# First feed-forward product of a hybrid attention block as a 2x2 block product with seven block multiplications

## The chip, the cores and the metric

The kernel runs on one NeuronCore of a Trainium2 chip (trn2). The metric is the device time of one execution in microseconds (us). Engines are named as in the profile: PE is the matrix engine (PEld its weight load), DVE the vector engine, ACT the scalar engine, POOL the GpSimd engine, SP the engine that only issues DMAs. All matmul operands are float32 or float32r (a float32 rounded to what PE multiplies in one pass).

## The reference, cut to what matters

One step of a block over 640 tokens (128 context tokens and 512 latent tokens) of width 1024: a mixer with two groups of heads, then a feed-forward part with a squared ReLU, then a final norm. Conditioning vectors give a shift, a scale and a gate per condition (context tokens have one, latent tokens the other).

```
h = rmsnorm(x, norm1_w) * (1 + sc1) + sh1
y, new_states = mixer(h, ...)                  # ends in a product with w_out
x = x + g1 * y
h = rmsnorm(x, norm2_w) * (1 + sc2) + sh2
x = x + g2 * (jnp.square(jax.nn.relu(h @ w_ff1)) @ w_ff2)   # w_ff1 1024x4096, w_ff2 4096x1024
out = rmsnorm(x, final_norm_w)
```

## The kernel before, in words

**Precision.** Each float32 matrix is held as a high part (rounded to float32r) and a low part (the rest). A product is three matmuls, high by high, high by low and low by high (`three`, lines 147 to 150). ACT makes the high part by a copy, DVE the low part by a subtraction (`split_l`, line 104). For weights this is done in `fetch` (121 to 139): an SP load of 512 KB into a staging tile `st` (two buffers), ACT writes `wh`, DVE writes `wl`. `weights` (141 to 145) runs that three tiles ahead of use, at high priority, over the list `todo` (109 to 118).

**Stages.** Until about 375 us the mixer; its last part is the product with w_out in four blocks of 256 output rows (loop at line 1011): each block's sums are added to the residual `xr` (1017), squared into `sq2` (1022) and scaled into `hH` and `hL` (1025, 1026), the high and low parts of the feed-forward input, 8 tiles k of 128 features by 640 tokens, plus two columns that hold the shift sh2 of the two conditions. The dots that give sh2 and later g2 are done by DVE (`ada_dot`, 961 to 969) on rows that POOL's queue loads.

**Feed-forward.** `ff1(f)` (1045 to 1065) makes tile f of 32 of the hidden layer: two PSUM banks, of 384 and of 258 columns, each with 8 k by 3 matmuls; DVE multiplies by the row norm `r2` (1057), ACT does ReLU with the shift as bias, the square and the high part, DVE the low part (1064). `ff2` (1098 to 1107) takes four hidden tiles at a time: for 5 token tiles by 2 halves one bank of 512 columns with 4 by 3 matmuls; `acc_y` (1109) adds each bank into `y` by DVE, 80 banks in all. At group 6 the sum is multiplied by g2 and added to the residual in token layout, `xt` (1116, 1117); group 7 goes through `last` (1120 to 1135), which also does the final norm and the stores. `to_tokens` (1074) turns the residual by PE transposes after tile 3.

**Order of the work.** The order on each engine comes from the framework's planner, which simulates the program and takes what is ready by priority; work marked high priority goes first. Each engine then runs its list strictly in order. Banks come from two pools, `bank` (3) and `xbank` (5 in this part). Weight tiles: 3 buffers each for high and low in `whp`, `wlp`, and 2 more of each in `whp2`, `wlp2` for the feed-forward part.

Of the kernel before, what the change touches and what calls it, by code (L numbers as in the profile page):

```python
# [19 lines left out]
P = 128  # L20
D = 1024
# [4 lines left out]
SPANS = ((0, 384), (384, 640))  # L26
CONDS = ((0, 0, P), (1, P, T))
# [23 lines left out]
def hybrid_step(ctx: ExitStack, tc: tile.TileContext, I, O):  # L51
# [909 lines left out]
    def ada_dot(g, ft, after=None):  # L961
        st = stp.tile([P, 1024], F32, tag="sta", name="stg")
        nc.gpsimd.dma_start(out=st, in_=I["adag"][0 if g == SH2 else 1, ft])
        for n in range(2):
            a = AB[:, g, ft, n:n + 1]
            i = stt(out=cr[:, 2, :], in0=st, scalar=1.0, in1=cr[:, n, :], op0=ALU.mult, op1=ALU.mult, accum_out=a)  # L966
            if after is not None:
                behind(i.ins, after)
            tt(out=a, in0=a, in1=cb[:, CB_BA + 8 * g + ft:CB_BA + 8 * g + ft + 1], op=ALU.add)
# [26 lines left out]
    sq2 = ffp.tile([P, T], F32, name="sq2")  # L996
# [8 lines left out]

    for k in range(KT):
        ada_dot(SH2, k)
        dve.tensor_copy(hH[:, k, T:T + 2], AB[:, SH2, k, :])
        split_l(hL[:, k, T:T + 2], AB[:, SH2, k, :], hH[:, k, T:T + 2])

    for b in range(4):
# [8 lines left out]
        for f in range(2):  # L1020
            k = 2 * b + f
            square_add(sq2, xr[:, k, :], k, 0, T)
            for c, p0, p1 in CONDS:
                a2 = AB[:, SC2, k, c:c + 1]
                act(hH[:, k, p0:p1], xr[:, k, p0:p1], AF.Copy, scale=a2)
                stt(out=hL[:, k, p0:p1], in0=xr[:, k, p0:p1], scalar=a2, in1=hH[:, k, p0:p1].bitcast(F32),
                    op0=ALU.mult, op1=ALU.subtract)
    r2 = ffp.tile([P, T], F32, name="r2")
    v2 = ffp.tile([P, T], F32, name="v2")
    for lo, hi in SPANS:  # L1030
        ps = xbank("ssq")
        sum_mm(ps, (sq2,), lo, hi)
        rstd_all(ps, r2, v2, sq2, lo, hi)
# [11 lines left out]
    def ff1(f):
        gh = ff.tile([P, T], F32R, tag="gh", bufs=6, name="gh")
        gl = ff.tile([P, T], F32R, tag="gl", bufs=6, name="gl")
        wh, wl = weights()
        u = ffp.tile([P, T], F32, tag="u", bufs=2, name="u")
        ub = sm.tile([P, 2], F32, tag="ub", name="ub")  # L1050
        for hf, (lo, hi) in enumerate(FSP):
            ps = (xbank if f < 4 and f % 2 else bank)("ff1")
            for k in range(KT):
                three(ps[:, 0:hi - lo], wh[:, k * P:(k + 1) * P], wl[:, k * P:(k + 1) * P],
                      hH[:, k, lo:hi], hL[:, k, lo:hi], k == 0, k == KT - 1)
            h_ = min(hi, T)
# [189 lines left out]
```

## Time and profile before

| | us |
|---|---|
| median of 3 runs | 839.74 |
| lowest and highest run | 837.88, 840.19 |
| the profiled execution, its own time | 838.31 |
| its span, first to last instruction | 836.5 |
| granted clock of PE, mean over the span | 0.991 of full speed |

The span is 1.81 us shorter than the time of the same execution; the rest lies before the first and after the last instruction. Busy times count an engine as busy while at least one of its instructions is in flight; matmuls overlap one another, so the mean duration of one matmul is longer than the distance between two.

### The profile page before, as it was taken

Reading aid. Unit: us, or ns where it says so; the run is one execution under the profiler, and the core shown is the slowest. Engines: PE = TensorE matmul, PEld = TensorE weight load, DVE = VectorE, ACT = ScalarE, POOL = GpSimd, SP = SyncE. Lnnn points to the kernel's source line nnn. Section 1 sums busy time; section 2 is a strip of 40 time slices with the busy share of each in tenths; the row PEclk is TensorE's granted clock in tenths of the full one; section 3 lists DMA queues with packets and bytes.
Section 4 is the critical chain, followed back from the end, with each engine's and each line's share of the span. In section 5 each row is a group of like instructions: output and inputs, shape, how many; then the busy total and the mean of one; then the engine's idle time right before and its main releaser. Section 6 shows DMA issues by size and latency. Waiting matters only on the chain.

```text
span 836.5 us, 14721 instructions
## 1 busy us (share of the span) xinstructions
PE 811.4 (97%) x6022; PEld 727.3 (87%) x6022; DVE 517.3 (62%) x1008; ACT 375.4 (45%) x734; POOL 62.4 (7%) x88
## 2 busy tenths in 40 slices
PE   6999999999999999999999999999999999999995
PEld 2787688999987899999989989899899898998984
DVE  4668897868565569997305837644254343447747
ACT  5456458466454576446624405226054052250432
POOL 1121000030253003000000000000000000000000
PEclk9899999999999999999999999999999999999998
DMA  9925424141252073564103415223042041230303
GB/s 347 356 78 189 166 79 152 52 127 53 64 139 64 2 252 102 166 197 142 52 25 126 153 48 158 96 76 101 26 127 76 8 144 50 76 102 26 101 1 126
DMA packets 28436, 92.50 MB, mean 111 GB/s; under 512 B 3649, under 2 KB 4561, under 8 KB 28113
## 3 DMA queue, kind: packets, MB, share of 16 engines
q1 hardware_dynamic: 21024, 71.61, 25.6%
q0 software_dynamic: 3936, 12.15, 5.3%
q10 hardware_dynamic: 3408, 7.80, 2.7%
q8 instruction: 47, 0.77, 0.4%
q14 instruction: 21, 0.16, 0.1%
HBM read 88.31 MB, written 3.20 MB: 109 GB/s over the span
## 4 chain that ended last, share of the span: by engine, by line
PE 87%; DVE 7%; ACT 2%; DMA 2%; issue 1%; SPq 0%; DVEq 0%; ACTq 0%
PE ff L150 18%; PE ff L148 18%; PE ff L149 18%; PE ada L233 2%; PE pt L150 2%; PE pt L149 2%; PE pt L148 2%; PE pn L894 2%; PE pn L899 1%; PE ob L150 1%; PE ob L149 1%; PE ob L148 1%; PE vb L150 1%; PE vb L148 1%; PE vb L149 1%
## 5 line engine op out<-in xcount | busy, mean ns | idle before, releaser
L83 ACT ACTIVATE wh<-st 128x1024 fp32r<-128x1024 f32 (+1 forms) x90 | 92.2, 1037 | 253.3 <-PE ff L150 134.5
L148 PE MATMUL ff<-hH,wh 128*128 128x258 f32 (+1 forms) x512 | 159.1, 311 | 0.0
L150 PE MATMUL ff<-hH,wl 128*128 128x258 f32 (+1 forms) x512 | 158.9, 311 | 0.0
L149 PE MATMUL ff<-hL,wh 128*128 128x258 f32 (+1 forms) x512 | 158.8, 310 | 0.0
L105 DVE TENSOR_TENSOR wl<-st,wh 128x1024 fp32r<-128x1024 f32 x86 | 105.7, 1232 | 80.7 <-ACT wh L83 80.2
L149 PE MATMUL ff<-wl,gh 128*128 128x512 f32 x320 | 124.6, 390 | 0.0
L148 PE MATMUL ff<-wh,gh 128*128 128x512 f32 x320 | 124.5, 389 | 0.0
L150 PE MATMUL ff<-wh,gl 128*128 128x512 f32 x320 | 124.3, 389 | 0.0
L149 PEld LDWEIGHTS ff<-hL,wh 128*128 128x128 f32 x512 | 96.6, 189 | 0.3
L148 PEld LDWEIGHTS ff<-hH,wh 128*128 128x128 f32 x512 | 96.3, 188 | 0.3
L150 PEld LDWEIGHTS ff<-hH,wl 128*128 128x128 f32 x512 | 96.5, 189 | 0.0
L1114 DVE TENSOR_TENSOR y<-ff,y 128x512 f32<-128x512 f32 x60 | 41.4, 691 | 78.2 <-PE ff L150 78.2
L150 PEld LDWEIGHTS ff<-wh,gl 128*128 128x128 f32 x320 | 60.1, 188 | 12.6
L148 PEld LDWEIGHTS ff<-wh,gh 128*128 128x128 f32 x320 | 60.1, 188 | 12.3
L149 PEld LDWEIGHTS ff<-wl,gh 128*128 128x128 f32 x320 | 60.1, 188 | 12.2
L1057 DVE TENSOR_TENSOR u<-ff,r 128x384 f32<-128x384 f32 x64 | 31.2, 488 | 48.4 <-PE ff L150 48.4
L149 PE MATMUL pt<-wl,hH 128*128 128x256 f32 x160 | 46.0, 288 | 0.2 <-DVE wl L105 0.2
L150 PE MATMUL pt<-wh,hL 128*128 128x256 f32 x160 | 45.6, 286 | 0.0
L148 PE MATMUL pt<-wh,hH 128*128 128x256 f32 x160 | 45.4, 286 | 0.0
L83 ACT ACTIVATE u<-u,ub 128x128 f32<-128x128 f32 x64 | 32.3, 552 | 19.9 <-DVE ub L1059 19.7
L105 DVE TENSOR_TENSOR gl<-u,gh 128x640 fp32r<-128x640 f32 x32 | 26.3, 823 | 22.9 <-ACT gh L83 22.8
L966 DVE SCALAR_TENSOR_TENSOR cr<-stg,cr 128x1024 f32<-128x1024 f32 x32 | 38.9, 1216 | 0.0
(361 smaller groups left out, 1613.3 us busy)
## 6 DMA issues: line engine op xcount, KB each, us to landing
st<-in_wff_dram SPq DMA_DIRECT2D x64, 512.0 KB, 3.5
sta<-in_ada_dram SPq DMA_DIRECT2D x32, 512.0 KB, 6.6
st<-in_win_dram SPq DMA_DIRECT2D x18, 512.0 KB, 3.7
stg<-in_adag_dram POOLq DMA_DIRECT2D x16, 512.0 KB, 3.8
st<-in_wout_dram SPq DMA_DIRECT2D x8, 512.0 KB, 3.6
xT<-in_xT_dram SPq DMA_DIRECT2D x8, 320.0 KB, 6.4
sb<-gdr POOLq DMA_DIRECT2D x20, 128.0 KB, 3.4
xr<-in_xT_dram ACTq DMA_DIRECT2D x8, 320.0 KB, 5.1
```

The costliest lines, as they stand in the source:

```text
L83: ins = nc.scalar.activation(out, in_, func, **kw)
L105: return (eng or dve).tensor_tensor(out=dst, in0=src, in1=hi.bitcast(F32), op=ALU.subtract)
L148: mm(out, lhsT=ah, rhs=bh, start=start, stop=False)
L149: mm(out, lhsT=ah, rhs=bl, start=False, stop=False)
L150: mm(out, lhsT=al, rhs=bh, start=False, stop=stop)
L233: mm(pa[32 * i:32 * i + 32, 0:n], lhsT=sc[:, 4 * rnd + i, :], rhs=sts[i // m][:, n * (i % m):n * (i % m) + n], start=(rnd == 0), stop=(rnd ...
L894: mm(o[h2], lhsT=sbs[z][:, (2 * h2 + p) * P:(2 * h2 + p + 1) * P], rhs=vb[:, c, 2 * p + h2, :], start=True, stop=(c == 0))
L899: mm(o[h2], lhsT=qw[r, z, p, (c - 1) * P:c * P], rhs=C[j][r, 2 * z + p, :], start=False, stop=True)
L966: i = stt(out=cr[:, 2, :], in0=st, scalar=1.0, in1=cr[:, n, :], op0=ALU.mult, op1=ALU.mult, accum_out=a)
L1057: tt(out=u[:, lo:h_], in0=ps[:, 0:h_ - lo], in1=r2[:, lo:h_], op=ALU.mult)
L1114: tt(out=y[:, c, s], in0=ps, in1=y[:, c, s], op=ALU.add)
```

## The change

The 1024x4096 matrix w_ff1 is cut in two along the input features and in two along the output features, and the input in two along the features and in two along the tokens (320 each, the upper half with the two shift columns). Hidden tiles p and p+16 form a pair. Instead of eight block products there are seven, with sums and differences of blocks as operands (Winograd's form of Strassen's scheme). `prod` is one of them: 4 k by 3 matmuls of 320 or 322 columns.

- **Input side.** The scaled input is first written as float32 (`hf`), then split; four combinations T1 to T4 are made by DVE differences over 4 tiles of 322 columns, each with a high part by ACT and a low part by DVE. T1 is made after the second block of the product with w_out, the others after the last.
- **Weight side, per pair.** `sums_of` loads both tiles and makes by DVE four sums of 512 columns; `unit` splits five of them (S1, S2, S3, A22, S4), each into a buffer of its own of which there is one. The two direct blocks A11 and A12 come by `direct`: a DMA from POOL that writes the rounded tile, an ACT copy with factor -1, and a second DMA that adds the loaded tile to it. For pair 0 they are made by ACT and DVE as before.
- **Products.** Three banks a, b, c per pair. Between products DVE (and once ACT) reads a bank whose sum then goes on growing: m2 after the first product into b, m3 after the second, and m3 again from c.
- **Second product.** `ff2` runs per pair, so a bank takes 2 by 3 matmuls instead of 4 by 3, and 160 banks are added into `y` instead of 80. Its weights are made by `second` from the same staging tiles and the same three weight buffers; `whp2` and `wlp2` are gone.
- **Start.** The first two products of pairs 0, 1 and 2 (`head`, and A12 by B21) come ahead of the norm's sum and of `to_tokens`.
- **Residual.** `to_tokens` stores to DRAM; after group 14 a POOL DMA adds it into `y`. `last` runs on `y`.
- **Small.** `ada_dot` writes its products as bfloat16 to a scratch tile in the feed-forward part, and the bias is added once per vector (`ada_bias`) instead of 16 times.

```
-    for f in range(32):
-        todo.append((I["wff1"][f], None))
-        if f % 4 == 0 and f > 0:
-            todo += [(I["wff2"][f - 4 + i], None) for i in range(4)]
-    todo += [(I["wff2"][28 + i], None) for i in range(4)]
...
+    def sums_of(p, out):
+        s1 = stp.tile([P, 1024], F32, tag="st", name="s1")
+        load(s1, I["wff1"][p])
+        s2 = stp.tile([P, 1024], F32, tag="st", name="s2")
+        load(s2, I["wff1"][p + 16])
...
+        s3 = stp.tile([P, 1024], F32, tag="sta", name="s3")[:, 0:512]
+        tt(out=s3, in0=s1[:, a], in1=s2[:, a], op=ALU.subtract)
+        tt(out=s2[:, a], in0=s2[:, a], in1=s2[:, b], op=ALU.add)
+        tt(out=s1[:, a], in0=s2[:, a], in1=s1[:, a], op=ALU.subtract)
+        tt(out=s1[:, b], in0=s1[:, b], in1=s1[:, a], op=ALU.subtract)
+        return [("S1", s2[:, a]), ("S2", s1[:, a]), ("S3", s3)], (s2[:, b], s1[:, b])
...
+    def unit(pool, name, src):
+        h = pool.tile([P, 512], F32R, tag=name + "h", name=name + "h")
+        l = pool.tile([P, 512], F32R, tag=name + "l", name=name + "l")
+        act(h, src, AF.Copy)
+        split_l(l, src, h)
+        return h, l
...
+    def direct(p):
+        with tc.high_priority():
+            wh = whp.tile([P, 1024], F32R, tag="wh", name="wh")
+            wl = wlp.tile([P, 1024], F32R, tag="wl", name="wl")
+            in_order(nc.gpsimd.dma_start(out=wh, in_=I["wff1"][p]))
+            act(wl, wh.bitcast(F32), AF.Copy, scale=-1.0)
+            in_order(nc.gpsimd.dma_start(out=wl, in_=I["wff1"][p], accum_op=ALU.add))
...
+    def prod(ps, A, B, start):
+        n = B[0].shape[2]
+        for k in range(4):
+            s = slice(k * P, (k + 1) * P)
+            three(ps[:, 0:n], A[0][:, s], A[1][:, s], B[0][:, k, :], B[1][:, k, :], start and k == 0, k == 3, skip=True)
...
+    def head(p, w):
+        a = xbank("pa") if p < 3 else bank("pa")
+        u = us[p % 3]
+        prod(a, w["A11"], B11, True)
+        act(u[:, LO], a[:, LO], AF.Copy)
+        return a, u
...
+    def ff1(p, w, early=None):
+        a, u = early or head(p, w)
...
+        first = [(b, "S2", T2), (c, "S1", T1)]
+        for ps, s, t_ in (first[::-1] if p == 0 else first):
+            prod(ps, w[s], t_, True)
+        tt(out=m2, in0=b[:, 0:HE], in1=u, op=ALU.add)
+        prod(b, w["S3"], T3, False)
+        tt(out=m3, in0=b[:, 0:HE], in1=u, op=ALU.add)
+        tt(out=m3, in0=c[:, 0:HE], in1=m3, op=ALU.add)
+        if not early:
+            prod(a, w["A12"], B21, False)
+            tt(out=z0[:, LO], in0=a[:, LO], in1=r2[:, LO], op=ALU.mult)
+        prod(c, w["S4"], B22, False)
+        tt(out=m2, in0=c[:, 0:HE], in1=m2, op=ALU.add)
+        tt(out=z0[:, HALF:T], in0=m2[:, LO], in1=r2[:, HALF:T], op=ALU.mult)
+        g0 = finish(z0, p, p, m2)
+        prod(b, w["A22"], T4, False)
+        tt(out=z1[:, HALF:T], in0=m3[:, LO], in1=r2[:, HALF:T], op=ALU.mult)
+        tt(out=z1[:, LO], in0=b[:, LO], in1=u[:, LO], op=ALU.add)
+        tt(out=z1[:, LO], in0=z1[:, LO], in1=r2[:, LO], op=ALU.mult)
+        g1 = finish(z1, p, p + 16, m3)
...
+    for p in range(3):
+        w = direct(p) if p else w0
+        a, u = head(p, w)
+        prod(a, w["A12"], B21, False)
+        heads[p] = (a, u)
...
+    for p in range(1, 17):
+        if p < 16:
+            w1 = {}
+            last_unit(w1, combined(p, w1))
+            if p >= 3:
+                w1.update(direct(p))
+            g[p] = ff1(p, w1, heads.get(p))
...
+        w2 = second(p - 1)
+        ff2(p - 1, g.pop(p - 1), w2, acc_y(p - 1) if p < 16 else last)
```

## Rows read from the trace of the kernel before

**Rows 1.** The page's head and part 1: busy us, share of the span, instructions.

```profile
span 836.5 us, 14721 instructions
PE 811.4 (97%) x6022; PEld 727.3 (87%) x6022; DVE 517.3 (62%) x1008; ACT 375.4 (45%) x734; POOL 62.4 (7%) x88
```

**Rows 2.** Busy time by stretch: us, busy (instructions) per engine, clock, DMA share, GB/s.

```profile
340.00:374.70 34.70, 34.70 (x241) 34.70 (x240) 33.32 (x85) 14.42 (x28) 3.17 (x6) 1.00 0.58 180
374.70:420.00 45.30, 45.30 (x306) 44.06 (x305) 25.23 (x46) 29.77 (x47) 0.00 (x0) 1.00 0.32 101
...
500.00:600.00 100.00, 100.00 (x575) 92.24 (x574) 52.80 (x91) 33.92 (x46) 1.06 (x2) 1.00 0.32 100
```

**Rows 3.** The page's chain that ended last, by line.

```profile
PE ff L150 18%; PE ff L148 18%; PE ff L149 18%; PE ada L233 2%; PE pt L150 2%; PE pt L149 2%; PE pt L148 2%; PE pn L894 2%; PE pn L899 1%; PE ob L150 1%; PE ob L149 1%; PE ob L148 1%; PE vb L150 1%; PE vb L148 1%; PE vb L149 1%
```

**Rows 4.** PE's timeline: start us, duration us; start of the feed-forward, and at 471.

```profile
374.69 0.33 PE L148 MATMUL ff<-hH,wh 128*128 128x384 f32 x1
...
377.85 0.28 PE L148 MATMUL ff<-hH,wh 128*128 128x258 f32 x1
...
379.89 0.29 PE L150 MATMUL ff<-hH,wl 128*128 128x258 f32 x1
...
471.23 0.40 PE L148 MATMUL ff<-wh,gh 128*128 128x512 f32 x1
...
475.80 0.39 PE L150 MATMUL ff<-wh,gl 128*128 128x512 f32 x1
```

**Rows 5.** DVE's groups, 374 to 836 us: count, busy us, mean ns, idle before.

```profile
L105 DVE TENSOR_TENSOR wl<-st,wh 128x1024 fp32r<-128x1024 f32 x62 | 75.6, 1223 | 62.0 <-ACT wh L83 61.7
L1114 DVE TENSOR_TENSOR y<-ff,y 128x512 f32<-128x512 f32 x60 | 41.4, 691 | 78.2 <-PE ff L150 78.2
L105 DVE TENSOR_TENSOR gl<-u,gh 128x640 fp32r<-128x640 f32 x32 | 26.3, 823 | 22.9 <-ACT gh L83 22.8
L966 DVE SCALAR_TENSOR_TENSOR cr<-stg,cr 128x1024 f32<-128x1024 f32 x16 | 19.5, 1218 | 0.0
L1057 DVE TENSOR_TENSOR u<-ff,r 128x384 f32<-128x384 f32 x32 | 17.8, 555 | 18.3 <-PE ff L150 18.3
L1057 DVE TENSOR_TENSOR u<-ff,r 128x256 f32<-128x256 f32 x32 | 13.5, 421 | 30.2 <-PE ff L150 30.2
```

**Rows 6.** DVE's timeline, 775 to 780 us: a bank read behind a weight split.

```profile
775.74 0.69 DVE L1114 TENSOR_TENSOR y<-ff,y 128x512 f32<-128x512 f32 x1 [0.58 <-PE ff L150]
...
777.80 1.22 DVE L105 TENSOR_TENSOR wl<-st,wh 128x1024 fp32r<-128x1024 f32 x1
778.94 0.68 DVE L1114 TENSOR_TENSOR y<-ff,y 128x512 f32<-128x512 f32 x1
779.54 1.22 DVE L105 TENSOR_TENSOR wl<-st,wh 128x1024 fp32r<-128x1024 f32 x1
```

**Rows 7.** The page's DMA issues: count, KB each, median us to landing.

```profile
sta<-in_ada_dram SPq DMA_DIRECT2D x32, 512.0 KB, 6.6
...
stg<-in_adag_dram POOLq DMA_DIRECT2D x16, 512.0 KB, 3.8
```

**Rows 8.** ACT's and DVE's timelines at the hand-over from w_out to the feed-forward.

```profile
369.84 1.06 ACT L83 ACTIVATE wh<-st 128x1024 fp32r<-128x1024 f32 x1 [2.12 <-PE woc L149]
...
377.36 0.71 ACT L83 ACTIVATE hH<-xr,AB 128x512 fp32r<-128x512 f32 x1
...
378.46 0.74 DVE L1026 SCALAR_TENSOR_TENSOR hL<-xr,AB,hH 128x512 fp32r<-128x512 f32 x1
```

**Rows 9.** Busy time by stretch at the end; columns as in rows 2.

```profile
799.60:808.60 9.00, 9.00 (x41) 7.44 (x41) 1.32 (x3) 2.50 (x4) 0.00 (x0) 1.00 0.01 2
808.60:826.95 18.35, 18.34 (x81) 14.84 (x80) 16.69 (x41) 7.40 (x26) 0.00 (x0) 1.00 0.23 86
826.95:836.50 9.55, 0.00 (x0) 0.00 (x0) 5.30 (x14) 1.21 (x5) 0.00 (x0) 0.71 0.29 110
```

**Rows 10.** DVE's timeline: the last instruction of the kernel on it.

```profile
831.77 1.42 DVE L1134 SCALAR_TENSOR_TENSOR xt<-xt,r_r,g2r 128x512 f32<-128x512 f32 x2
```

More of the change, by code (lines that the diff above doesn't have):

```diff
@@ L959, in silu_rows, with ada_dot @@
         return cr
-    def ada_dot(g, ft, after=None):
+    def ada_dot(g, ft, cr, junk, after=None):
         st = stp.tile([P, 1024], F32, tag="sta", name="stg")
@@ L1022, in hybrid_step @@
             square_add(sq2, xr[:, k, :], k, 0, T)
+            hk = hf[k // 4][:, k % 4, :]
             for c, p0, p1 in CONDS:
[L1024 to L1027, printed above, removed]
-    r2 = ffp.tile([P, T], F32, name="r2")
[L1029 to L1033, printed above, removed]
@@ L1034, in hybrid_step @@
-    opst.close()
+                act(hk[:, p0:p1], xr[:, k, p0:p1], AF.Copy, scale=AB[:, SC2, k, c:c + 1])
+            n = HALF if k < 4 else T
+            act(hH[:, k, 0:n], hk[:, 0:n], AF.Copy)
+            split_l(hL[:, k, 0:n], hk[:, 0:n], hH[:, k, 0:n])
+        if b == 1:
+            t1 = first_difference()
+        if b == 3:
+            with tc.high_priority():
+                w0 = {}
+                first = sums_of(0, w0)
+    r2 = ffp.tile([P, T], F32, name="r2")
+    v2 = ffp.tile([P, T + 4], F32, name="v2")
@@ new lines, in combined, with last_unit @@
+    def combined(p, out):
+        with tc.high_priority():
+            order_, rest = sums_of(p, out)
+            for name, src in order_:
+                out[name] = unit(sp, name, src)
+        return rest
+    def last_unit(out, src):
+        with tc.high_priority():
+            out["A22"] = unit(ff, "A22", src[0])
+            out["S4"] = unit(ff, "S4", src[1])
+    with tc.high_priority():
+        for name, src in first[0]:
+            w0[name] = unit(sp, name, src)
+    s4 = first[1]
@@ L1041, in hybrid_step @@
-    FSP = ((0, 384), (384, T + 2))
-    splits = []
[L1045 to L1056, printed above, removed]
-            tt(out=u[:, lo:h_], in0=ps[:, 0:h_ - lo], in1=r2[:, lo:h_], op=ALU.mult)
-            if hf == 1:
-                dve.tensor_copy(ub, ps[:, T - lo:T + 2 - lo])
-        for c, p0, p1 in CONDS:
-            act(u[:, p0:p1], u[:, p0:p1], AF.Relu, bias=ub[:, c:c + 1])
-        act(u, u, AF.Square)
-        act(gh, u, AF.Copy)
-        splits.append(split_l(gl, u, gh).ins)
-        return gh, gl
@@ L1067, in hybrid_step, with in_order @@
-    cr = ff.tile([P, 3, 1024], F32, tag="rows", name="cr")
-    nc.scalar.dma_start(out=cr[:, 0:2, :], in_=crd.unsqueeze(0).to_broadcast([P, 2, D]))
-    xt = ff.tile([P, NT, D], F32, name="xt")
-    def wide(name):
-        return ff.tile([P, 512], F32, tag="wide", bufs=2, name=name)
+    assert not todo and not ready
+    issued = []
+    def in_order(ins):
+        if issued:
+            behind(ins.ins, issued[-1])
+        issued.append(ins.ins)
+    def direct(p):
+        with tc.high_priority():
+            wh = whp.tile([P, 1024], F32R, tag="wh", name="wh")
+            wl = wlp.tile([P, 1024], F32R, tag="wl", name="wl")
+            in_order(nc.gpsimd.dma_start(out=wh, in_=I["wff1"][p]))
+            act(wl, wh.bitcast(F32), AF.Copy, scale=-1.0)
+            in_order(nc.gpsimd.dma_start(out=wl, in_=I["wff1"][p], accum_op=ALU.add))
+        w = [(wh[:, 512 * i:512 * i + 512], wl[:, 512 * i:512 * i + 512]) for i in range(2)]
+        return {"A11": w[0], "A12": w[1]}
@@ new lines, in second @@
+    def second(p):
+        out = []
+        with tc.high_priority():
+            for f in (p, p + 16):
+                st = stp.tile([P, 1024], F32, tag="st", name="st2")
+                load(st, I["wff2"][f])
+                wh = whp.tile([P, 1024], F32R, tag="wh", name="wh")
+                wl = wlp.tile([P, 1024], F32R, tag="wl", name="wl")
+                act(wh, st, AF.Copy)
+                split_l(wl, st, wh)
+                out.append((wh, wl))
+        return out
+    def prod(ps, A, B, start):
[3 more added lines that the diff above has]
+            three(ps[:, 0:n], A[0][:, s], A[1][:, s], B[0][:, k, :], B[1][:, k, :], start and k == 0, k == 3, skip=True)
@@ L1096, in cond, with ff2 @@
         return 0 if c == 0 else 1
-    def ff2(g, gs, evac):
-        w = [weights() for i in range(4)]
+    def ff2(g, gs, w, evac):
         for c in range(NT):
```

153 lines of the change are left out of this document (111 added, 42 removed).

## Prediction

> **What bounds the kernel now.** I start with the page's busy line: PE is busy 97% of the span, DVE 62%, ACT 45% [rows 1]. A share over the whole span says nothing of one stage, so the busy times by stretch come next: from 374.7 to 420 us PE is busy for all 45.3 us, and from 500 to 600 us for all 100, at full clock, with DVE at 53% [rows 2]. In the w_out stage before it DVE is nearly full as well (33.3 of 34.7 us) and PE still never stops [rows 2]. The chain that ended last is PE's feed-forward matmuls for 54% of the span [rows 3]. So from 374.7 us to the end of the matmuls at about 826.95 the time is the number of matmuls times the distance between two of them, and that distance must be read from starts, not durations. On PE's timeline 18 matmuls of 384 columns lie between 374.69 and 377.85, so 0.1756 us each; 17 of 258 columns between 377.85 and 379.89, 0.120 us each; 20 of 512 columns between 471.23 and 475.80, 0.2285 us each [rows 4]. Check: 32 tiles x 24 x (0.1756 + 0.120) = 227.0 us and 960 x 0.2285 = 219.4 us make 446.4 of the 452.3 us; the norm's sums and the transposes fill the remaining 5.9. There is no idle time to win, only work to remove, and each matmul removed is worth its full distance as long as PE stays fed.
>
> **The removed matmuls.** The first product had 32 x 2 x 24 = 1536 matmuls; it gets 16 pairs x 7 x 12 = 1344, of 320 or 322 columns. No row has that width. Between the rows of 258 and 384 columns, 320 gives 0.120 + 62/126 x 0.0556 = 0.1474 us and 322 gives 0.1482; with three products of the one and four of the other the mean is 0.148 [rows 4]. So 1344 x 0.148 = 198.9 us against 227.0: **28.1 us less**. The bounds are the two rows themselves at equal cost per column (0.457 and 0.465 ns): 197.1 to 200.6, a saving of 26.4 to 29.9. The second product keeps 960 matmuls of 512 columns, and the transposes stay.
>
> The Trainium skill (TensorE: Matmul & The Clock Gate, "Back-to-back issue gap") gives N/2.4 + 2.5 ns between matmuls, 216 ns for 512 columns where the rows show 228; as an estimate by that page the saving would be 26.1 us and the sum 2 us higher. The row decides, since it holds what these float32r streams really do.
>
> **DVE in the steady part.** What the removed matmuls cost is on DVE. The mean of a 1024-column split is 1.223 us, of a 512-column read of a bank 0.691 [rows 5]. Back to back they take about 0.08 us less: a split started at 777.80 and the next operation, a read, at 778.94, so 1.14, and the one after it at 779.54, so 0.60 [rows 6]. Per pair: four sums and five splits of 512 columns, 9 x 0.60 = 5.4; two splits of w_ff2 tiles, 2.3; nine reads and products of 320 columns at about 0.40 (between 0.421 and 0.555 less 0.08), 3.6; two splits of 640 columns at 0.74, 1.5; ten banks added to y, 6.0, twice as many as before per hidden tile. That is 18.8 us, and 21.2 in the eight pairs with an `ada_dot` (2 x 1.22) [rows 5, 6]. PE needs 84 x 0.148 + 60 x 0.2285 = 26.1 us per pair. DVE goes from 53% to 72 to 81%: not the bound by throughput. ACT's splits, reads and ReLUs per pair cost less than DVE's and nobody reads a bank through ACT but for u, with three products between; I cost them at nothing; if ACT fell behind, the weights would be late next.
>
> **The new waits on DVE.** Before, PE never needed DVE except to free one of eight banks. Now S3 by T3 may start only when DVE has read b for m2, and S4 by B22 only when DVE has made both steps of m3. One product of 12 matmuls, 1.78 us, lies in between each time. m2 needs 0.4 to 0.5 plus whatever DVE is in the middle of: a read that PE had ready at 775.74 + 12 x 0.2285 = 778.48 started at 778.94, behind a split [rows 6]. With one such split ahead (up to 1.22) m2 ends at 1.7, just covered; m3 needs about 0.9, so 2.1 in that case, 0.3 late. Behind a waiting matmul stands all of PE. If there is never a split ahead the wait is 0, if two long operations stand ahead of each read it is about 1 for m2 and 1.4 for m3. The planner puts weight splits first, but they are few (a 1.14 us split twice in 26 us), so I take 0.2 us a pair, **3 us**, with bounds 0 and 16 (1 us a pair) in the range.
>
> **Weight buffers.** The steady loop has one buffer per combined block and three weight tiles. A direct block's tile is free after A12 by B21 of the pair before; then come two products (3.6 us) and a second product (13.7), 17.3 us in all, for POOL's DMA, ACT's copy of 1.06 and the adding DMA. No row shows a DMA that rounds or adds. The nearest is POOL's plain load of the same 512 KB, 3.8 us; the longest 512 KB row is 6.6, from the crowded start [rows 7]. The copy's 1.06 is a row as well [rows 8]. Two at 3.8 with the copy make 8.7, two at 6.6 make 14.3: hidden at both ends. The staging tiles go round within about 16 of the 26.1 us by the same prices. Free at both ends, then, with 3 us in reserve at the worse.
>
> **The start.** Before, the feed-forward began 0.1 us after the last w_out matmul on features that were ready, and the last input split ended at 379.2 [rows 8]; tiles 0 to 4 could all run ahead. Now pair 0 has 12 matmuls on ready features and 6 more on tiles 4 and 5 (2.7 us); transposes and S1 by T1 can fill, if the planner places them there. An extra ACT copy of 0.7 stands in the chain to the last split, so B21 is whole at about 380. Pair 1's weight tile comes free in the middle of the last w_out block (ACT's next use of one waited for that until 369.84 [rows 8]), so it is ready at about 379; pair 2's at the end of the block, 374.7 + 8.7 + 1 for the issues = 384.4, or 390 at the slow price. PE's work up to the first product on T2 is 72 + 12 matmuls and the 5.9 us of the balance above, 18.3 us, so until 393; DVE's (the old work left after 374.9, three differences and three splits of 1288 columns at 1.43, sums and splits, 8 operations of the norm) comes to some 22 us, ending at 397, of which the first parts are the urgent ones. Pairs 0 to 2 also lack A12 by B21 as a cover: two reads of about 0.9 us for m3 each, and 0.5 for m2 in pair 0, are exposed, 3.2 us. If second products or transposes fill all of this the cost is 0; if pair 2 and T2 come late as well, 9. I take 3.2 + 1.8 = **5 us**.
>
> **The tail.** The last second product had 120 matmuls, and DVE's work on its banks (scaling, adding, the norm) fitted beside them: from the first finished bank at 808.6 DVE was busy 16.69 + 5.30 = 22.0 us, ending at 833.19 [rows 9, 10]. Now the last product has 60 matmuls, 13.7 us, and the same 22.0 us on DVE. With its start as zero, the first bank ends at 1.4 (banks one after the other) or 4.1 (the first halves of five banks taken first, since the second weight tile is free only as the product before ends); then 22.0, then about 0.9 idle in the last norm and 3.3 from the last DVE operation to the end of the span. The end comes at 27.6 to 30.3, that is 13.9 to 16.6 after the last matmul, against 9.55 now: 4.4 to 7.1 us, I take **5.5**.
>
> **The sum.** 838.31 - 28.1 + 3 + 5 + 5.5 = 823.7 for the profiled execution. The median is 1.4 higher, so **825** for the runs. A measurement of this kernel can tell about 0.3%, 2.5 us, from no change.
>
> **The rivals.**
> - *All but the tail is hidden.* The planner has fillers for every gap, since it already mixes tiles when k 6 and 7 are late. 838.31 - 28.1 + 4.4 = 814.6, 816 on the median's scale; 812 at the upper saving of 29.9. For it: PE's unbroken 45.3 us at the old start [rows 2]. Chance 0.22.
> - *The start and the first pairs cost 9 us and the steady waits 7.* 838.31 - 28.1 + 9 + 7 + 5.5 = 831.7, or 833. The steady loop fills only after the first two pairs, each load waiting for the buffer before. Chance 0.13.
> - *DVE is late in every pair, and the kernel is slower.* The place is m2 and m3: each read behind a run of weight sums or splits (high priority, four sums in a row are 2.4 us). With 1.8 us a pair, 29 us, the time is 838.31 - 28.1 + 29 + 10.5 = 849.7, or 851. It decides from (28.1 - 10.5)/16 = 1.1 us a pair on. For it: the 0.46 us by which a read came late at half the load [rows 6]. Against: 5 us of DVE in each 26 are free. The Trainium skill (PSUM — Partial Sum Buffer, "Engine vs sequencer instructions") calls VectorE's queue strict FIFO; the trace agrees, as no read overtakes a split there. Chance 0.15, of which 0.05 end within 2.5 us of no change.
> - *The adding DMA is slow.* At 10 us each, the chain of a direct block is 21 + 1 for issues, 4.8 us beyond its 17.3, in 13 pairs: 62 us, 888. No row speaks for it. Chance 0.05.
>
> **How the numbers follow.** The forecast keeps 0.45, with its own range 819 to 831. Faster: 0.22 + 0.13 + 0.45 = 0.80; same 0.05; slower 0.15. The range starts at 813, near the lower end of the first rival, and ends at 843, where the bounds of the start (9), the steady waits (16) and the tail (7.1) meet: 838.31 - 28.1 + 32.1 + 1.4 = 843.7.
>
> **What would show it.** The chain should still be PE, with 1344 matmuls of 320 and 322 columns 0.148 us apart. PE's idle time before S3 and S4 products, put down to m2 and m3, should total some 3 us from pair 3 on and 3 in the first pairs. DVE should be at 72 to 81% of a stretch in the middle, and the span should end 14 to 17 us after the last matmul. PE idle on `wl` of a direct block would prove the buffers' sum wrong; over 1.1 us idle a pair on m2 or m3 would prove the forecast wrong altogether; a distance well above 0.148 would take the saving itself.

## The result, and the profile after

The changed kernel takes **843.98 us** (median of 5 runs, 843.51 to 844.67) against 839.74 for the kernel before beside it: ratio 1.0055, 95% interval 1.004 to 1.007. It is slower by 4 us where I forecast 15 us faster, and it lies 1 us above the range of 813 to 843. The profiled execution has a span of 842.4 us and took 844.21.

The page's head, part 1 and the chain by line, beside [rows 1, 3]:

```profile
span 842.4 us, 14750 instructions
...
PE 798.6 (95%) x5830; PEld 704.8 (84%) x5830; DVE 641.9 (76%) x1200; ACT 416.3 (49%) x827; POOL 88.3 (10%) x123
...
PE ff L145 9%; PE ff L146 8%; PE ff L147 8%; PE pb L145 3%; PE pb L147 3%; PE pb L146 3%; PE pc L145 2%; PE pc L146 2%; PE pa L147 2%; PE pc L147 2%; PE pa L145 2%; PE pa L146 2%; PE pt L146 2%; PE pt L147 2%; PE pt L145 2%
```

The matmuls went (6022 to 5830 is exactly the 192), PE was 13 us less busy, and the span still grew. So PE no longer worked all the time. The busy times by stretch, columns as in rows 2 and 9, say where:

```profile
374.70:400.00 25.30, 15.79 (x87) 14.70 (x86) 20.71 (x29) 17.82 (x28) 2.33 (x3) 0.85 0.37 89
400.00:420.00 20.00, 16.80 (x104) 15.45 (x104) 8.09 (x16) 8.47 (x16) 0.00 (x0) 0.93 0.55 205
420.00:450.00 30.00, 29.95 (x148) 25.62 (x147) 19.27 (x30) 19.24 (x32) 0.55 (x1) 0.95 0.46 144
500.00:600.00 100.00, 100.00 (x540) 89.08 (x539) 81.87 (x137) 42.76 (x67) 7.87 (x12) 1.00 0.49 140
...
826.46:842.40 15.94, 0.00 (x0) 0.00 (x0) 12.83 (x37) 4.40 (x16) 0.00 (x0) 0.59 0.43 164
```

Where PE had been busy for all 45.3 us at clock 1.00 [rows 2], it now works 32.6 of 45.3, and the granted clock falls to 0.85, 0.93 and 0.95 in the three stretches. In the steady part PE is full, with DVE at 82%. After the last matmul come 15.94 us, where it was 9.55 [rows 9].

PE's timeline names the waits. These are all of them up to the end of the matmuls, then some rows to read distances from:

```profile
375.23 0.31 PE L147 MATMUL pa<-hH,wl 128*128 128x320 f32 x1
...
382.04 0.44 PE L147 MATMUL pa<-hH,wl 128*128 128x320 f32 x1 [4.87 <-DMA wl<-in_wff_dram]
...
385.48 0.41 PE L145 MATMUL pa<-hH,wh 128*128 128x320 f32 x1
...
391.34 0.42 PE L147 MATMUL pa<-hH,wl 128*128 128x320 f32 x1 [1.12 <-DMA wl<-in_wff_dram]
...
397.49 1.11 PE L1221 MATMUL xT<-kb,xr 128*128 128x128 f32 x4 [3.52 <-DVE u L1161]
...
409.76 0.41 PE L145 MATMUL pb<-tHL,S3h 128*128 128x322 f32 x1 [0.58 <-DVE sq L1192]
...
412.41 0.42 PE L145 MATMUL pb<-tHL,A22h 128*128 128x320 f32 x1 [0.58 <-DVE sq L1194]
...
418.84 0.41 PE L147 MATMUL pc<-hH,S1l 128*128 128x322 f32 x1 [1.98 <-DVE S1l L107]
...
606.12 0.40 PE L145 MATMUL ff<-wh,g 128*128 128x512 f32 x1
...
609.63 0.39 PE L145 MATMUL ff<-wh,g 128*128 128x512 f32 x1
...
826.06 0.40 PE L147 MATMUL ff<-wh,g 128*128 128x512 f32 x1
```

Three things are to be seen. **The waits** add up to 12.65 us, all before 420. **The clock**: 13 distances between 382.04 and 385.48 take 3.44 us, 0.265 each, where 0.148 is usual; the granted clock is at its lower level, 1.2 instead of 2.4 GHz, for some microseconds at and after the end of each of the three long waits (4.87, 3.52 and 1.98 us). **The second product**: 15 distances between 606.12 and 609.63 take 3.51 us, 0.234 each; before, 0.2285 stood in rows 4. The mean over the stretch from 450 to 820, worked out from all starts of matmuls that follow one another there, is 0.2335 now and 0.2270 before. Nothing in that stretch waits, so this is the same matmul taking longer.

From the first matmul behind the product with w_out to the end of the last matmul is the **stage**: 452.25 us before, 451.23 after (two matmuls of pair 0 had already run at 365.07). From there to the end of the span is the **tail**. The removed matmuls are worth -28.1, the distance of the second product 960 x 0.0065 = +6.2, the waits +12.65; 8.2 are left to balance. Adding up, from the starts of all matmuls before 450 that did not wait, what each distance exceeds the usual one of its kind by gives 7.9 us, where the kernel before has 0.4: 5.6 of it stands in the stretches at the lower clock, 2.3 in short delays beside them. With the tail's +6.4 and a 0.5 us later start this is the 5.9 us of span.

The queues behind the waits: DMA issues (count, KB, median us to landing), then rows of POOL's, ACT's, DVE's and SP's timelines.

```profile
wh<-in_wff_dram POOLq DMA_DIRECT2D x15, 512.0 KB, 3.8
wl<-in_wff_dram POOLq DMA_DIRECT2D x15, 512.0 KB, 5.6
...
376.07 0.90 POOL L1136 DMA_DIRECT2D wl<-in_wff_dram  x1 [4.67 <-DVE xr L1053]
376.63 0.89 POOL L1134 DMA_DIRECT2D wh<-in_wff_dram  x1
...
374.71 1.06 ACT L85 ACTIVATE wl<-wh 128x1024 fp32r<-128x1024 f32 x1 [3.26 <-DMA wh<-in_wff_dram]
375.67 1.26 ACT L85 ACTIVATE hH<-t 128x1288 fp32r<-128x1288 f32 x1
...
376.97 1.50 DVE L107 TENSOR_TENSOR hL<-t,hH 128x1288 fp32r<-128x1288 f32 x1 [0.66 <-ACT hH L85]
...
382.87 1.55 DVE L107 TENSOR_TENSOR hL<-hfP,hH 128x640 fp32r<-128x640 f32 x2
...
396.95 0.48 DVE L1188 TENSOR_TENSOR z<-pa,r 128x320 f32<-128x320 f32 x1
...
398.23 8.40 SPq L1223 DMA_DIRECT2D xtd<-xq  x5
406.74 2.01 SPq L98 DMA_DIRECT2D s<-in_wff_dram  x2
```

The adding DMA takes 5.6 us where the load that only rounds takes 3.8. Pair 2's load was issued at 376.63, right behind pair 1's adding DMA. ACT stood 3.26 us before the copy of pair 1's tile, with the high part of the first difference, whose input was ready, queued behind it. DVE read pair 0's bank, which the transposes needed next, only at 396.95 (the row of the wait names a small DVE instruction right behind that read). Pair 1's loads stood on SP behind the five stores of the residual.

### The profile page after: what moved, and what is told of

It is laid out like the page before. It is cut to its first block, busy times and chain, and to the rows that moved or that the text cites. A ratio compares the mean times of both kernels' runs of the same rounds, so it can differ in the third digit from the quotient of the medians.

```text
span 842.4 us, 14750 instructions
## 1 busy us (share of the span) xinstructions
PE 798.6 (95%) x5830; PEld 704.8 (84%) x5830; DVE 641.9 (76%) x1200; ACT 416.3 (49%) x827; POOL 88.3 (10%) x123
## 4 chain that ended last, share of the span: by engine, by line
PE 80%; DVE 10%; DMA 4%; ACT 3%; issue 2%; DVEq 0%; POOL 0%; SPq 0%; ACTq 0%; POOLq 0%
PE ff L145 9%; PE ff L146 8%; PE ff L147 8%; PE pb L145 3%; PE pb L147 3%; PE pb L146 3%; PE pc L145 2%; PE pc L146 2%; PE pa L147 2%; PE pc L147 2%; PE pa L145 2%; PE pa L146 2%; PE pt L146 2%; PE pt L147 2%; PE pt L145 2%
## 5 line engine op out<-in xcount | busy, mean ns | idle before, releaser
L146 PE MATMUL ff<-wl,g 128*128 128x512 f32 x320 | 126.2, 396 | 0.0
L147 PE MATMUL ff<-wh,g 128*128 128x512 f32 x320 | 125.7, 395 | 0.0
L145 PE MATMUL ff<-wh,g 128*128 128x512 f32 x320 | 123.0, 396 | 0.1
L1256 DVE TENSOR_TENSOR y<-ff,y 128x512 f32<-128x512 f32 x140 | 94.0, 683 | 13.4 <-PE ff L147 13.1
L107 DVE TENSOR_TENSOR wl<-st,wh 128x1024 fp32r<-128x1024 f32 x54 | 65.9, 1235 | 28.7 <-ACT wh L85 28.6
L147 PEld LDWEIGHTS ff<-wh,g 128*128 128x128 f32 x320 | 60.0, 188 | 14.2 <-DVE g L107 0.4
L146 PEld LDWEIGHTS ff<-wl,g 128*128 128x128 f32 x320 | 60.0, 188 | 12.7 <-DVE wl L107 0.3
L145 PEld LDWEIGHTS ff<-wh,g 128*128 128x128 f32 x320 | 59.9, 188 | 12.8 <-ACT g L85 0.3
L147 PE MATMUL pa<-hH,wl 128*128 128x320 f32 x128 | 41.2, 322 | 6.0 <-DMA wl<-in_wff_dram 6.0
L145 PE MATMUL pa<-hH,wh 128*128 128x320 f32 x128 | 41.3, 324 | 0.0
L146 PE MATMUL pa<-hL,wh 128*128 128x320 f32 x128 | 41.0, 320 | 0.0
L963 DVE SCALAR_TENSOR_TENSOR cr<-stg,cr 128x1024 f32<-128x1024 f32 (+1 forms) x32 | 38.9, 1216 | 0.1
```

Source lines behind the costliest of these rows:

```text
L107: return (eng or dve).tensor_tensor(out=dst, in0=src, in1=hi.bitcast(F32), op=ALU.subtract)
L145: mm(out, lhsT=ah, rhs=bh, start=start, stop=False, skip_group_check=skip)
L146: mm(out, lhsT=ah, rhs=bl, start=False, stop=False, skip_group_check=skip)
L147: mm(out, lhsT=al, rhs=bh, start=False, stop=stop, skip_group_check=skip)
L963: i = stt(out=junk, in0=st, scalar=1.0, in1=cr[:, n, :], op0=ALU.mult, op1=ALU.mult, accum_out=a)
L1256: tt(out=y[:, c, s], in0=ps, in1=y[:, c, s], op=ALU.add)
```

## The experiments

All are measured against the kernel before on the same chip. Since the starting time of the stage differs by up to 2 us between executions of identical work (373.65 to 375.60 in these runs), I compare stages and tails beside the ratios. They are those of one profiled execution each, and the executions of one kernel differ by up to 4.4 us (best: 830.70 to 835.08), so less than a microsecond of stage tells nothing by itself. The "spacing" of the expectations is the distance of this text.

| run | us | ratio to before | stage | tail |
|---|---|---|---|---|
| before (profile shown) | 839.74 | | 452.25 | 9.55 |
| after | 843.98 | 1.0055 (1.004 to 1.007) | 451.23 | 15.94 |
| align | 840.06 | 1.0024 (1.001 to 1.0037) | 447.87 | 16.1 |
| align_mod256 | 839.24 | 1.0012 (1.0004 to 1.0021) | 446.47 | 16.2 |
| before_pairs | 847.4 | 1.0108 (1.0093 to 1.0123) | 453.24 | 17.1 |
| before_shift | 842.04 | 1.0045 (1.0031 to 1.0059) | 456.76 | 9.6 |
| start_dve | 843.48 | 1.0066 (1.0051 to 1.0081) | 450.71 | 16.0 |
| xt_banks | 839.56 | 1.0018 (1.0007 to 1.003) | 446.30 | 16.0 |
| start | 838.73 | 1.0005 (0.9996 to 1.0014) | 445.60 | 16.0 |
| start2 | 830.93 | 0.9914 (0.99 to 0.9927) | 439.15 | 16.0 |
| tail | 842.6 | 1.0057 (1.0044 to 1.0071) | 456.88 | 10.2 |
| best | 833.25 | 0.994 (0.9923 to 0.9956) | 448.01 | 9.6 |
| best2 | 826.85 | 0.9867 (0.9847 to 0.9887) | 439.22 | 10.5 |
| best3 | 827.01 | 0.9865 (0.9848 to 0.9882) | 440.19 | 10.3 |

### The distance in the second product

**align** moves the tiles of the pool that holds g by 32 bytes:

```diff
-    us = [..., ff.tile([P, HE], F32, name="u3")]
+    us = [..., ff.tile([P, HE + 8], F32, name="u3")[:, 0:HE]]
```

> The changed kernel with one tile (u3) made 32 bytes longer, so that the tiles behind it, the relu outputs g and the weight units A22 and S4, start where the corresponding tiles started before the change (an odd multiple of 32 bytes instead of a multiple of 64). Nothing else changes. Theory A (the spacing of 0.2335 us against 0.227 in the 512-column products comes from where the tiles lie): spacing back to 0.227, 960 x 0.0065 = 6 us less, 838 us. Rival B (it comes from banks of 6 matmuls where there were 12): spacing stays 0.2335, time stays 844.

The mean distance fell to 0.2295 and the stage by 3.4 us: theory A for the larger part, though not down to 0.227.

**before_pairs** gives the kernel before the other candidate alone, banks of 6 matmuls:

```diff
...
-                for k in range(4):
+                for k in range(2):
...
-        if f % 4 == 0 and f > 0:
-            ff2(f // 4 - 1, gs[0:4], acc_y(f // 4 - 1))
-            del gs[0:4]
+        if f > 3 and f % 2 == 0:
+            for j in ([0, 1] if f == 4 else [f // 2 - 1]):
+                ff2(j, gs[0:2], acc_y(j))
+                del gs[0:2]
```

> The kernel before, its second product made for 2 tiles at a time instead of 4: 6 matmuls a bank and 160 additions on VectorE instead of 80, the first product untouched. Rival B (6 matmuls a bank slow the spacing): 0.2335 in place of 0.227, 6 us, and with them the longer tail that two tiles a bank leave (VectorE bound: last matmul to end 16 instead of 9.5 us), so 839.7 + 6 + 6 = 852. Theory A (where the tiles lie): spacing stays 0.227, only the tail is longer: 846. If neither holds, 840.

The distance came to 0.2279: the banks are worth 0.0009 at most, 0.9 us. Rival B falls. The tail grew from 9.6 to 17.1 us, with nothing else of the change in the kernel, so the longer tail is the two-tile banks' doing. That is the loss here: 7.5 of 8 us of span.

**align_mod256** pads u3 by 96 bytes (`HE + 24`):

> The changed kernel with u3 96 bytes longer instead of 32, so that g starts at the same place within 256 bytes as the weights it is multiplied with (160), as it did before the change. The 32-byte shift took the spacing of the 512-column products from 0.2335 to 0.2293 us, not all the way to 0.227. Theory A2 (the place within 256 bytes matters too): 0.227 to 0.228, 837 to 838. Theory A1 (only an odd against an even multiple of 32 bytes matters; the rest is the banks of 6 matmuls, which in the kernel before by pairs came to 0.2278): 0.229, 839 to 840, as the 32-byte shift.

The mean was 0.2284, the stage 446.47. It lies between the two numbers, and the ratio's interval overlaps that of align: this run does not tell A1 and A2 apart. **before_shift** is the reverse, in the kernel before:

```diff
-    xt = ff.tile([P, NT, D], F32, name="xt")
+    xt = ff.tile([P, NT * D + 8], F32, name="xt")[:, 0:NT * D].rearrange("p (c d) -> p c d", d=D)
```

> The kernel before with one tile 32 bytes longer, so that its relu outputs (the stationary operands of the second product) start at a multiple of 64 bytes, as in the changed kernel; nothing else is changed. Theory A (the place of the stationary tile alone sets the spacing of the 512-column products): 0.227 becomes 0.232 to 0.234, 960 x 0.006 = 6 us, ratio 1.005 to 1.008. Rival (the spacing in the changed kernel needs its one tile for both parts of g, or its banks of 6 matmuls, as well): spacing and time as before, ratio 0.998 to 1.002.

The mean rose from 0.2270 to 0.2316, and the stage by 4.5 us (960 x 0.0046 = 4.4); the ratio, 1.0045, is just under the 1.005 to 1.008 of theory A. PE's timeline of align_mod256, then of before_shift; 15 distances lie between the two rows of each:

```profile
603.63 0.40 PE L145 MATMUL ff<-wh,g 128*128 128x512 f32 x1
...
607.05 0.40 PE L145 MATMUL ff<-wh,g 128*128 128x512 f32 x1
```

```profile
599.82 0.40 PE L148 MATMUL ff<-wh,gh 128*128 128x512 f32 x1
...
603.31 0.40 PE L148 MATMUL ff<-wh,gh 128*128 128x512 f32 x1
```

3.42 us and 3.49 us, so 0.228 and 0.2327. In both directions, then, 32 bytes in the place of the tiles are worth 0.004 to 0.005 us on each of 960 matmuls. Shown is that the place of the tiles of that pool counts; g is the only one of them that both experiments moved and that these matmuls read.

The trace of before_shift says more, since there the weights come from two places: `whp2` and `wlp2` lie behind the pool of g and moved with it, `whp` and `wlp` did not. By the addresses that the framework gives the tiles, the weights of the second product start 160 bytes past a multiple of 256 in all five kernels of the table below, and 192 bytes past one only in `whp2` and `wlp2` of before_shift. The table gives these places for weights and g, and the mean distances from all starts of the second product in before_shift, from the stretch 450 to 820 elsewhere:

| kernel | weights | g | us |
|---|---|---|---|
| before | 160 | 160 | 0.2270 |
| align_mod256 | 160 | 160 | 0.2284 |
| before_shift, whp2 | 192 | 192 | 0.2294 |
| align | 160 | 96 | 0.2295 |
| before_shift, whp | 160 | 192 | 0.2335 |
| after | 160 | 64 | 0.2335 |

So g's place alone does not decide, as theory A and A1 have it: at 192 it is slow with the one kind of weights and not with the other. In these six rows the distance is long where the two operands lie an odd number of 32 bytes apart, and shorter where the number is even. No run was made to test that by itself. The combined blocks A22 and S4 moved in align as well, and the distance of their products stayed at 0.147 to 0.149.

### The start

**start_dve** replaces the adding DMA for pairs 1 and 2:

```diff
-            in_order(nc.gpsimd.dma_start(out=wl, in_=I["wff1"][p], accum_op=ALU.add))
+            if p < 3:
+                tt(out=wl, in0=wh.bitcast(F32), in1=wl.bitcast(F32), op=ALU.add)
+            else:
+                in_order(nc.gpsimd.dma_start(out=wl, in_=I["wff1"][p], accum_op=ALU.add))
```

> The changed kernel, low parts of pairs 1 and 2 by a VectorE addition instead of a second DMA that adds: theory S (the adding DMA, 6 us from issue to landing and queued ahead of the next load, is what the start waits for): the idle stretches of 4.87 and 1.12 us before heads 1 and 2 shrink to under 1.5 together, and the half-clock stretch behind the first of them goes, 5 to 8 us off, 836 to 839. Rival V (VectorE, full from 379 to 398, is the bound of the start whatever the DMA does; two more additions of 1.1 us make it later): the wait moves to the transposes and the products behind, 842 to 845.

The two DMA waits went, and the stage gained 0.5 us. The time came back at once as waits on DVE, 1.53, 2.09 and 4.86 us among them. Rival V, for this edit: behind the first late link stood the next one.

**xt_banks** takes on two other links:

```diff
-            pt = xbank("xT")
+            pt = bank("xT")
...
-        nc.sync.dma_start(out=xtd[c], in_=t_[:, 0:D])
+        nc.scalar.dma_start(out=xtd[c], in_=t_[:, 0:D])
```

> The changed kernel, the transposes of the residual in the other three PSUM banks and their stores on ScalarE's queue instead of SyncE's; the adding DMAs stay. Theory Q (the 3.5 us wait of the transposes for pair 0's bank and the 2.0 us wait for pair 1's sums, whose loads stood behind the stores on SyncE, are each removed): idle before 420 falls from 12.7 to about 7, 836 to 839. Rival V (VectorE's queue decides when bank a and the T2 and T4 parts are ready): the idle time shows up at another matmul and the time stays 842 to 845.

The stage fell by 4.9 us, although the waits only fell from 12.65 to 10.81; the rest is in the distances before 450, whose excess fell from 7.9 to 5.0. That is nearer to theory Q than to V in the time (839.56, above its 836 to 839), but not in the idle time that Q gave. Two rows of PE's timeline show what is left:

```profile
381.71 0.63 PE L147 MATMUL pa<-hH,wl 128*128 128x320 f32 x1 [3.07 <-DMA wl<-in_wff_dram]
...
413.61 0.64 PE L145 MATMUL pc<-hH,S1h 128*128 128x322 f32 x1 [5.21 <-ACT S1h L85]
```

With the transposes free to move, 12 of them now fill part of the first wait. Pair 1's loads were issued at 400.66, when the splits of pair 0 freed the staging tiles, and were there only at 408.6, the stores of the residual beside them; that is the 5.21.

**start** adds two more edits: staging tiles of the other pair of buffers for pair 1, and GpSimd instead of the adding DMA.

```diff
+        q1, q2 = ("sta", "st") if p == 1 else ("st", "sta")
-        s1 = stp.tile([P, 1024], F32, tag="st", name="s1")
+        s1 = stp.tile([P, 1024], F32, tag=q1, name="s1")
...
+                nc.gpsimd.tensor_tensor(out=wl, in0=wh.bitcast(F32), in1=wl.bitcast(F32), op=ALU.add)
```

> The changed kernel with three edits at its start: transposes in the other banks and stores on ScalarE's queue as in the run before this (837.7 span), low parts of pairs 1 and 2 by a GpSimd addition instead of the adding DMA, and pair 1's two tiles loaded into the other pair of staging buffers, so that they do not wait for pair 0's last splits. Theory Q (each of these waits is a link of its own): the waits of 3.07 and 5.21 us left in that run shrink to under 1 each; idle between 375 and 420 under 4 us, span 829 to 832. Rival V (VectorE's work of 20 us between 379 and 401 is the bound of what remains): idle of 6 or more shows up at the products that need T4, S4 or bank a; span 834 to 837.

A miss for Q: 0.7 us of stage, 9.59 of idle left and a span of 837.2 us, which is close to V's numbers. Two reasons are in its rows, first of GpSimd's and then of DVE's timeline:

```profile
376.09 2.39 POOL L1138 TENSOR_TENSOR wl<-wh,wl 128x1024 fp32r<-128x1024 f32 x1 [4.32 <-ACT wl L85]
...
383.39 3.16 POOL L1138 TENSOR_TENSOR wl<-wh,wl 128x1024 fp32r<-128x1024 f32 x1 [4.37 <-ACT wl L85]
```

```profile
377.21 2.64 DVE L107 TENSOR_TENSOR hL<-t,hH 128x1288 fp32r<-128x1288 f32 x1 [0.53 <-ACT hH L85]
...
384.25 3.72 DVE L107 TENSOR_TENSOR hL<-hfP,hH 128x640 fp32r<-128x640 f32 x2
```

The DVE subtractions beside the two additions took 2.64 instead of 1.50 us and 3.72 instead of 1.55; the DVE rows between them kept their usual length. The Trainium skill (SBUF — State Buffer, "SBUF: two separate sides") says that GpSimd and VectorE share one pair of ports, held for a whole instruction, when the VectorE operation has two inputs in SBUF. These rows agree: each row of subtractions began while a GpSimd addition ran and ended 1.4 us after it, about its usual length. The other reason: the loads of pair 1 now stood on SP behind the broadcast load of `cr`, which was issued only at 398.83, when its memory came free.

**start2** mends both, and lets ACT make the first difference before it waits for pair 1's tile:

```diff
-    nc.sync.dma_start(out=cr, in_=crd.unsqueeze(0).to_broadcast([P, 2, D]))
+    nc.gpsimd.dma_start(out=cr, in_=crd.unsqueeze(0).to_broadcast([P, 2, D]))
...
-            act(wl, wh.bitcast(F32), AF.Copy, scale=-1.0)
+            i = act(wl, wh.bitcast(F32), AF.Copy, scale=-1.0)
+            if p == 1:
+                behind(i.ins, t1_high)
...
-                nc.gpsimd.tensor_tensor(out=wl, in0=wh.bitcast(F32), in1=wl.bitcast(F32), op=ALU.add)
+                tt(out=wl, in0=wh.bitcast(F32), in1=wl.bitcast(F32), op=ALU.add)
```

> As the run called start, but the low parts of pairs 1 and 2 are added on VectorE (the GpSimd additions made VectorE's subtractions beside them 2.63 instead of 1.50 us and 3.72 instead of 1.56), ScalarE makes the high part of the first difference before it waits for pair 1's load, and the broadcast load that stood ahead of pair 1's loads on SyncE goes to GpSimd's queue. Theory Q' (what is left are queue places again): idle between 375 and 420 from 9.6 to 3 to 6 us, span 830 to 834 (start: 837.2). Rival V (VectorE's own work until 401 sets it): idle 8 or more, span 836 to 839.

Q' holds, with a span of 829.2 us a little below its 830; and V falls, since DVE has two additions more to do here. The stage is 439.15 us, 12.1 below the changed kernel's. The stretches of busy time, then all waits of PE up to 420:

```profile
375.00:400.00 25.00, 20.09 (x116) 18.96 (x115) 23.53 (x33) 15.11 (x25) 0.53 (x1) 0.86 0.27 71
400.00:420.00 20.00, 19.34 (x130) 18.41 (x130) 16.64 (x30) 14.81 (x28) 0.00 (x0) 1.00 0.68 254
```

```profile
378.08 0.41 PE L145 MATMUL pa<-hH,wh 128*128 128x320 f32 x1 [0.81 <-DMA wh<-in_wff_dram]
...
389.69 0.64 PE L145 MATMUL pc<-hH,S1h 128*128 128x322 f32 x1 [3.42 <-DVE rt L169]
...
396.60 0.39 PE L145 MATMUL pb<-tHL,S3h 128*128 128x322 f32 x1 [0.68 <-ACT xq L85]
...
413.05 0.41 PE L145 MATMUL pb<-tHL,A22h 128*128 128x320 f32 x1 [0.66 <-DVE sq L1200]
```

5.57 us of idle are left, 7.1 less, and one long wait instead of three. The other 5.0 us of the 12.1 came without an idle row: the excess of the distances before 450 fell from 7.9 to 3.2 us, of which the stretches at the lower clock hold 2.5 instead of 5.6 (the granted clock is 1.00 from 400 to 420, where it was 0.93). What each of the edits gave by itself is not told apart.

### The tail, and the version that beats both

**tail** makes the last two pairs' second products as one of 4 tiles, so 12 matmuls a bank; the first halves of five banks are taken first. The fourth weight tile lies in the space of S1 and S2.

```diff
-        w2 = second(p - 1)
-        ff2(p - 1, g.pop(p - 1), w2, acc_y(p - 1) if p < 16 else last)
+        if p < 15:
+            ff2(p - 1, g.pop(p - 1), second(p - 1), acc_y(p - 1))
+    gs, w = [*g[14], *g[15]], second(14) + second(15)
...
+    pss = [xbank("ff2") for j in range(5)]
+    for j in range(5):
+        half(*at[j], pss[j], 0)
+    for j in range(5):
+        half(*at[j], pss[j], 2)
+        last(*at[j], slice(512 * at[j][1], 512 * at[j][1] + 512), pss[j])
...
```

> The changed kernel with the last two pairs (14 and 15) in one second product of 4 tiles, as before the change: 12 matmuls a bank at the end, so VectorE's work for a bank fits beside it. The same matmuls, 10 fewer additions. Theory T (the tail is longer because a bank of two tiles takes TensorE 1.4 us and VectorE over 2.4): from the last matmul to the end 9 to 11 us instead of 15.9, time 844 - 6 = 838. Rival: VectorE still carries work from pair 15 into the last product, or the fourth weight tile comes late: tail 13 or more, 841 to 844.

PE's timeline around the last pair, and the end by stretch:

```profile
804.26 0.31 PE L147 MATMUL pc<-hH,S4l 128*128 128x322 f32 x1
808.20 0.80 PE L145 MATMUL ff<-wh,g 128*128 128x512 f32 x1 [3.63 <-ACT g L85]
808.80 0.63 PE L146 MATMUL ff<-wl,g 128*128 128x512 f32 x1
809.22 0.63 PE L145 MATMUL ff<-wh,g 128*128 128x512 f32 x1
```

```profile
830.93:841.10 10.17, 0.00 (x0) 0.00 (x0) 7.01 (x21) 2.26 (x8) 0.00 (x0) 0.72 0.54 206
```

Theory T holds for the tail, 10.2 us, and the gain was given back ahead of it. The planner had used up the first halves inside the last pair; behind it PE stood idle for 3.63 us, waiting for the last relu output, and went on at 0.43 us a matmul instead of 0.234. The stage grew by 5.6 us. I had counted on the halves as cover and not written down where they must stand.

**best** is align_mod256, start and tail together.

> All of it together: the tiles at the same place within 256 bytes as before the change, the three edits of the start, and the last two pairs in one second product. If the causes are separate their gains add: 842.4 less 3 to 6 (spacing), less 9 to 13 (start), less 6 (tail): span 818 to 825, faster than the kernel before by 1.4 to 2.2%. If they share a cause (VectorE at 82% busy takes up what is freed), less than the sum: 826 to 832.

At 832.4 us of span it beats the kernel before, but by less than the sum, and just above the 826 to 832 of the second forecast: the idle behind the last pair (3.66 us here) and the misses of start are in it. **best2** takes start2 instead of start and holds all five halves back until the last first-product matmul; **best3** holds three.

```diff
+            if k == 0 and at.index((c, n)) in held:
+                for e in ends[-2:]:
+                    behind(m[0], e)
```

> The run called best with the start of start2 and with the first halves of the last product's five banks held until the last first-product matmul is issued: in best they were used up earlier, and TensorE then idled 3.66 us for the last relu output and ran at half clock for 5 us after it. If that idle was only a matter of order: 832.4 less 5 to 6, less what start2 gains on start: span 820 to 826. If the halves were needed where they stood (as cover for waits inside the last pair), 829 to 832.

> As best2, but only three of the five first halves are held back (4.1 us of cover after the last pair instead of 6.8, two halves left as cover inside it). If the last relu output needs about 5.5 us from the last matmul (3.66 idle in best after none, with the evictions still to come), 1.4 us idle and some half-clock work remain: 2 to 4 us slower than best2; if best2 idles inside the last pair instead, faster than it by 1 to 3.

```profile
783.35 0.44 PE L145 MATMUL pc<-hH,S4h 128*128 128x322 f32 x1 [2.35 <-DVE sq L1208]
```

```profile
389.32 0.42 PE L145 MATMUL pc<-hH,S1h 128*128 128x322 f32 x1 [3.42 <-DVE rt L169]
...
783.62 0.64 PE L145 MATMUL pb<-tHL,A22h 128*128 128x320 f32 x1 [4.10 <-DVE sq L1207]
...
375.00:400.00 25.00, 18.16 (x120) 17.04 (x120) 23.90 (x33) 14.71 (x25) 0.53 (x1) 1.00 0.28 78
```

The first row is of best2's PE timeline, the others are of best3: two of its PE timeline, then a stretch of busy time. From 420 on best2 waits 2.35 us, and 0.59 before that, inside the last pair, where the halves had been cover; best3 has one wait of 4.10 us there, before A22 by T4. Both forecasts of the order were only half right: the idle moved forward, and shrank in best2 alone, and holding two halves fewer changed nothing that these intervals tell. The start of the two shows something else: start2, best2 and best3 have the same long wait there, 3.42, 3.40 and 3.42 us, but the granted clock from 375 to 400 was 0.86, 0.93 and 1.00. The lower clock does not follow every such wait. At **826.85 us, ratio 0.9867 (0.9847 to 0.9887)**, best2 is 1.3% faster than the kernel before and, by the two ratios (0.9867 to 1.0055), 1.9% faster than the change as it came.

## Why the prediction was wrong

- *The removed matmuls*: right. 1344 matmuls, 0.148 us apart on the mean.
- *DVE in the steady part*: right, 82% of the stretch from 500 to 600 against 72 to 81, and no wait of PE on it there.
- *The new waits on DVE*: 3 us forecast, 0 measured. From 420 on PE never waited for m2 or m3. The planner put A12 by B21 and then 16 matmuls of a second product (606.12 to 609.63 above) between S1 by T1 and S3 by T3 in the pair shown, a cover that my sum, with one product between a read and its user, had left out. The two rivals with late steady waits fall with it.
- *Weight buffers*: right in the steady part, where a landing of 5.6 us was always hidden. The sign that I had set against it, PE idle on `wl` of a direct block, came only in the start, at 382 and 391.
- *The start*: **the step that failed.** 5 us forecast, bounds 0 to 9; 21 measured: 12.65 us of idle, 5.6 of matmuls at the lower clock, and some 2.6 of short delays and of what the balance leaves open. Of the 3.2 us that I had set for exposed reads of m2 and m3, 1.16 came (the two waits of 0.58); the rest is elsewhere, and three parts of the sum were wrong. Pair 1's low part came at 382 instead of 379, its adding DMA taking 5.9 us where I had 3.8, and pair 2's at 391 instead of 384 to 390: I had let both pairs' DMAs start as their buffers came free, but the kernel issues them from POOL in one order, so pair 2's load waited for pair 1's adding DMA. I let the transposes fill, and they stood behind a bank that DVE held until 397. And I costed no moved instruction by its queue: the stores ahead of the loads on SP, the copy ahead of the difference on ACT. start2, which only reorders queues, banks and buffers and adds on DVE, takes 12.1 us off the stage; 8.8 of the 21 are still in it. The lower clock was no term at all.
- *The second product's distance*: a term that was missing. I kept 960 x 0.2285 as it was; it became 0.2335 from 0.2270, 6.2 us. The tiles' new place is 4.9 of it (align_mod256), banks of 6 matmuls up to 0.9 (before_pairs); the small rest is open.
- *The tail*: right, 6.4 us against 5.5, bounds 4.4 to 7.1. before_pairs shows the cause by itself, and tail removes it.

Put together: 16 us more in the start, 6 in the second product and 1 in the tail, less 3 in the steady part, make 20 us, and 823.7 forecast against 844.2 for the profiled execution is 20.5. That the result lies only 1 us above the range, and 0.3 above the 843.7 that its bounds add up to, is luck: the range's upper end held 16 us for steady waits, which never came, and the start took 16 more than its 5. The mechanism that carried the forecast, fewer matmuls on a full PE, was right, and best2, with much of the three losses taken back, comes to 826.85 us. That is no test of the 825, which had the longer tail in it.

## What to carry to other kernels

Where a change saves work on an engine that never stops, price its start by walking each queue in order for the first two or three rounds: what is first issued, what stands behind it, and which bank or staging tile it needs; then allow for time at the lower clock after long waits, which most of them brought here and one of 3.42 us did not. A fully hidden steady part says nothing about the first 45 us. And after a change of tile sizes, compare the place of the operands in SBUF with the place before, as well as the distance of matmuls that were not touched.

## What was not expected of the hardware

- 32 bytes in the place of a stationary tile changed the mean distance of 512-column matmuls from 0.2270 to 0.2316 us in one kernel, and from 0.2335 to 0.2295 in the other; in the first it was 0.2335 with weights that had stayed in place and 0.2294 with weights that had moved along.
- An accumulating DMA of 512 KB took 5.6 us in the median where one on the same queue that only rounds took 3.8.
- A VectorE subtraction of 1288 columns took 2.64 us beside a GpSimd addition instead of 1.50, and the GpSimd additions of 1024 columns took 2.39 and 3.16 us where VectorE's operations of that size take 1.22 [rows 5].
